# Where a norm weight is multiplied in: weight rows or transposed activations, in a two-layer decoder trunk

## The chip, the cores and the metric

One core of a Trainium2 chip runs the whole trunk in one launch. The metric is the device time of that core in microseconds. The engines are TensorE (PE, its weight loads PEld), VectorE (DVE), ScalarE (ACT), GpSimd (POOL) and SyncE (SP), which only issues DMAs here.

## The reference, cut to what matters

256 tokens of width 2048 pass two layers. Each sub-layer is `x += RMSNorm(f(RMSNorm(x)))`: a mixer (one input projection, attention in 8 + 8 heads of two kinds, one output projection) and a SwiGLU with 5632 hidden columns.

```python
def rms_norm(x, w):
    y = x * lax.rsqrt(jnp.mean(x * x, axis=-1, keepdims=True) + NORM_EPS)
    return y * w

for layer in range(2):
    u = rms_norm(h, mix_norm_pre[layer])
    u = mixer(u)                       # u @ w_in, two kinds of attention, @ w_out
    h = h + rms_norm(u, mix_norm_post[layer])
    u = rms_norm(h, ffn_norm_pre[layer])
    u = (silu(u @ w_gate) * (u @ w_up)) @ w_down
    h = h + rms_norm(u, ffn_norm_post[layer])
```

A norm in front of a projection is a factor per token (the rsqrt) and a weight per input column. `(x * r * w) @ W` is `r * (x @ (w * W))`, with w down the rows of W, and as well `r * ((x * w) @ W)`.

## The kernel before, in words

The 256 tokens are two tiles of 128. A projection takes the activations as the stationary operand, transposed to [128 k, 128 tokens], and streams weights past them as [128 k, 512 columns]. The products are exact to float32: both operands are split into a high part (rounded to float32r) and a low part (what is left), and `step` (L201 to L214) issues three matmuls per k tile, xh*wh (L208), xh*wl (L209), xl*wh (L210).

Weights come in pieces of two k tiles, 512 KB, one DMA on SP's queue each (`load_until`, L187 to L199). There are 808 of them: 120 in the first input projection (16 of these narrow, 272 or 256 columns), 96 in the second, 32 in each output projection, 528 in the two feed-forwards, of which 176 are of the down projection. For each k tile of a piece `split` (L177 to L184) makes the high part on ACT and the low part on DVE. Where the projection has a norm ahead of it (input, gate and up projections: 568 pieces) the norm weight, a column `nw` of one value per partition, is multiplied in on both engines (L183, L184); otherwise the plain forms are used (L180, L181). Raw pieces have 4 buffers, split pieces 10 (WB).

`transposed` (L251) makes the left operand of a normed projection: PE transposes a [128, 512] chunk of the residual into PSUM (L175), and one plain split of 512 columns follows (L180, L181, seen as m<-p). It runs for 8 chunks at the start, and from `post_residual` (L293) for 4 chunks of each tile at three turns: output projection to feed-forward (twice) and first feed-forward to second input projection. The factor per token (`prenorm_factor`, L260) is applied to the product.

Order of the work: `run_phase` (L231) emits pieces for tile 0 and tile 1 in turn, tile 1 some 4 pieces behind, 8 at both ends of a phase, so that what lies between two projections of one tile can run while PE works on the other. The attention arithmetic is cut into generators, whose steps are emitted between pieces (`advance`). Over this order a scheduler in the framework (`schedule_with_timeline_sim=True`, in `kernel`) plans each engine's own order by a timing model; on the chip every engine then keeps its order, and waits on semaphores.

Of the kernel before, what the change touches and what calls it, by code (L numbers as in the profile page):

```python
"""Two-layer hybrid decoder trunk (stick-breaking + gated DeltaNet, MoBA + dilated, SwiGLU) on one core.

Every projection runs on the tensor engine in float32r with both operands split exactly into a high
and a low part (x = xh + xl, w = wh + wl); xh*wh + xh*wl + xl*wh accumulate in float32 PSUM.
The activations are the stationary operand, transposed, [128 k, 128 tokens]; the weights stream past as
[128 k, 512 columns].  A norm in front of a projection costs no pass over the activations: its weight
goes into the rows of the projection as they are split, its factor into the product.
The 256 tokens are two tiles of 128; the second follows the first some weight pieces behind, so what
lies between two projections of one tile runs while the tensor engine works on the other.  The
attention arithmetic is emitted in small steps between weight pieces.  # L10
"""
# [6 lines left out]
F32R = mybir.dt.float32r  # L18
# [26 lines left out]
class Step:  # L45
    """One weight piece ([128, 2 k tiles, up to 512 columns]) and where it is used.  norm: the norm whose
    weight, one value per row of the piece, goes into it."""

    def __init__(self, src, kts, chunk, first, last, norm):
        self.src, self.kts, self.chunk, self.first, self.last, self.norm = src, kts, chunk, first, last, norm  # L50
        self.wh = self.wl = None


class Chunk:
    def __init__(self, pieces, lhs, done, norm=None):
        self.lhs, self.done = lhs, done
        self.acc = [None, None]
        n = len(pieces)
        self.steps = [Step(s, k, self, i == 0, i == n - 1, norm) for i, (s, k) in enumerate(pieces)]
# [9 lines left out]
class Pool:  # L69
    """Equal places handed out and returned in the order of the trace, each as a new tile.  # L70
    Requests of the generators are served in turn."""
# [26 lines left out]
    def renew(self, a):  # L98
        """The same place as a new tile."""
        return self.at(self.place.pop(id(a))[1])  # L100


def v4(t):
    """[128, 512] -> [128, 4, 128]"""
    return t.rearrange("p (h d) -> p h d", d=P)


class Builder:
# [23 lines left out]
    def now(self, pool, n=1):  # L132
        """Tiles for work that is emitted in one go."""
        while len(pool.free) < n:
            assert self.advance(), "no tile becomes free"
        return pool.pop(n)

    def bc(self, col, n=P):
        """[128, h] columns -> [128, h, n] with stride 0 on the last axis."""
        return col.unsqueeze(2).broadcast_to([P, col.shape[1], n])  # L140

    def rep(self, m, h=4):
        """[128, n] -> [128, h, n] with stride 0 on the middle axis."""
        return m.unsqueeze(1).broadcast_to([P, h, m.shape[1]])

    def rsqrt(self, v, n, tag):
        """v ** -0.5 for a [128, n] tile: a power and one Newton step, as two factors."""
# [12 lines left out]
    def rms(self, ss):  # L160
        """Sums of squares of four column chunks, and D * EPS beside them -> rms ** -1 as two factors."""
# [10 lines left out]
    def transpose4(self, o, src):  # L172
        """[128, 4, 128] -> [128, 512] with each [128, 128] block transposed."""
        for j in range(4):
            self.nc.tensor.transpose(o[:, j * P:(j + 1) * P], src[:, j, :], self.ident)  # L175

    def split(self, h, l, src, scale=None):  # L177
        """src (float32), times a column if there is one -> h (its float32r part) and l (what is left of it)."""
# [8 lines left out]
    def load_until(self, n):  # L187
        nc = self.nc
        while self.loaded < min(n, len(self.steps)):
# [5 lines left out]
            for j, kt in enumerate(s.kts):  # L195
                scale = None if s.norm is None else self.nw[:, s.norm * KT + kt:s.norm * KT + kt + 1]
                self.split(wh[:, j], wl[:, j], raw[:, j], scale)
# [18 lines left out]
    def advance(self):  # L216
        """Emits the next stage of each piece of attention work that can go on."""
# [13 lines left out]
    def run_phase(self, lo, hi, end):  # L231
        """Tile 1 follows LAG_EDGE pieces behind at both ends of a phase and LAG pieces in between."""
# [16 lines left out]
    # A norm in front of a projection: its weight is multiplied into the rows of the projection, its  # L249
    # factor (one per token) into the product.  # L250
    def transposed(self, t, c):  # L251
        """Column chunk c of the residual, transposed and split, as left operand."""
# [3 lines left out]
        self.split(h.bitcast(F32R), l.bitcast(F32R), o)  # L256
# [16 lines left out]
    def norm_weight(self, w, which, layer, c):  # L273
        """Columns of a norm weight, the same on every partition."""
# [18 lines left out]
    def post_residual(self, t, last):  # L293
        """x += y * rsqrt(mean(y^2)); y already holds the weight."""
# [6 lines left out]
        for c in range(4):  # L301
# [3 lines left out]
            if last:  # L305
                nc.sync.dma_start(out=self.out[t * P:(t + 1) * P, c * 512:(c + 1) * 512], in_=x)
            else:
                self.transposed(t, c)
        self.y[t] = None
        if not last:  # L310
# [6 lines left out]
    def run(self):  # L317
# [23 lines left out]
        for c in range(4):  # L341
            for t in range(2):
                self.transposed(t, c)
# [8 lines left out]
    def warm_up(self):  # L352
        """Products of zeros, until the first operands have arrived: the tensor engine's clock rises with use."""
# [15 lines left out]
    def ld_r(self, name, w):  # L369
        """w matrices of 0, 1 and -1 as float32r, which holds them exactly."""  # L370
# [25 lines left out]
    def col_chunk(self, w, c, done, norm):  # L396
        return Chunk([(w[c, p], (2 * p, 2 * p + 1)) for p in range(KT // 2)], self.lhs_a, done, norm)

    def plan_even_in(self):
# [5 lines left out]
        for g in range(2):  # L405
            for kind in (0, 1, 3, 2):
                if g == 0 and kind == 3:
                    chunks.append(self.col_chunk(self.I["ev_w_abz"], 0, lambda t, acc: self.abz_chunk(t, acc), 0))
                    chunks.append(self.col_chunk(self.I["ev_w_z"], 0, lambda t, acc: self.z_chunk(t, 0, 2, acc), 0))
                    continue  # L410
                done = lambda t, acc, g=g, kind=kind: self.gdn_chunk(t, g, kind, acc)
                chunks.append(self.col_chunk(w, c, done, 0))
                c += 1
            for kind in range(3):
                done = lambda t, acc, g=g, kind=kind: self.attn_chunk(t, 0, g, kind, acc)
                chunks.append(self.col_chunk(w, c, done, 0))
# [3 lines left out]
    def plan_odd_in(self):  # L420
        chunks = []
        for c in range(12):
            g, kind = c // 3, c % 3
            done = lambda t, acc, g=g, kind=kind: self.attn_chunk(t, 1, g, kind, acc)
            chunks.append(self.col_chunk(self.I["od_w_in"], c, done, 1))
# [16 lines left out]
    def plan_ffn(self, layer):  # L442
        chunks, waiting = [], []
        g, u, d = self.I["ffn_w_gate"], self.I["ffn_w_up"], self.I["ffn_w_down"]
        for q, grp in enumerate(FFN_GROUPS):
# [6 lines left out]
            for i, f in enumerate(grp):  # L452
                chunks.append(self.col_chunk(g[layer], f, lambda t, acc: self.gate_chunk(t, acc), 2 + layer))
                if i == 0:
                    chunks += waiting
                chunks.append(self.col_chunk(u[layer], f, lambda t, acc, i=i: self.up_chunk(t, i, acc), 2 + layer))
# [51 lines left out]
    def end_ffn(self, t, layer):  # L508
        self.post_residual(t, layer == 1)
# [40 lines left out]
    def end_out(self, t, layer):  # L550
        self.post_residual(t, False)

# [38 lines left out]
    def stick(self, t, g):  # L591
        """Weights are built transposed, [key, (head, query)]; the suffix sums over keys are products
        with triangular and all-ones matrices of the split terms."""
# [48 lines left out]
    def softmax_attn(self, t, g):  # L642
        """Causal softmax attention; the mask adds the logarithm of how often a key counts."""
# [51 lines left out]
    def abz_chunk(self, t, acc):  # L695
        """Columns a, b and the first two heads of z."""
# [31 lines left out]
    # The tokens of the second two heads of a group are in reverse order (flipped) in k, v and all that  # L728
    # is indexed like them: what is lower triangular in the first two heads is upper triangular there, and
    # one matrix holds both for the inverse.  Queries and outputs are in natural order throughout.  # L730
    def gdn_gates(self, t, ab):
        """The decay logs g [128, 8] split, beta [128, 8], exp of the prefix (tile 1) or suffix (tile 0) sums
        of g, and the prefix sums again in natural order."""
# [35 lines left out]
    def gdn_decay(self, t, g):  # L769
        """exp(sum of g over (k, c]) as [c, (head, k)] for k < c and as [k, (head, c)] for k <= c."""  # L770
# [30 lines left out]
    def gdn_conv(self, t, g, kind, nat):  # L801
        """Causal 4-tap convolution with the channels on partitions."""
# [6 lines left out]
        # heads, the columns of their tokens, of the taps before this tile and of the tile's last tokens  # L809
# [296 lines left out]
```

## Time and profile before

| | |
|---|---|
| time, median of 3 runs | 2433.02 us (2432.94 to 2434.01) |
| span of the profiled execution, first to last instruction | 2436.3 us, 3.3 us over that median |
| mean granted TensorE clock | 0.994 of full speed |
| PE busy | 2407.8 us |
| DVE busy | 1470.4 us |
| ACT busy | 1291.9 us |
| POOL busy | 194.7 us |
| chain of work that ended last | PE 94%, DVE 2%, ACT 1%, POOL 1%, DMA 1% |

Of the profiled execution the page gives its span as the only time; no other is listed for it. "Busy" is the time in which an engine runs at least one instruction. In a row of instructions, `out<-in` are tile names with buffer numbers left out: `wh`, `wl` are the high and low parts of a weight piece, `raw` the loaded piece, `m` one of the general [128, 512] tiles, `p` a PSUM tile, `acc` the accumulator of a projection, `nw` the norm weights. What stands behind the bar or in brackets is the idle time before and what ended it.

### The profile page before, as it was taken

What the parts mean: (1) busy time and instruction counts of PE and PEld (TensorE: products, weight loads), DVE (VectorE), ACT (ScalarE), POOL (GpSimd) and SP (SyncE); (2) the same over time, 40 slices, a digit from 0 to 9 for tenths busy, and PEclk for the clock granted to TensorE, in tenths of its full rate; (3) what the DMA queues carried; (4) which work ended last, traced back from release to release, by engine and by line L of the source; (5) the groups of instructions that cost most, each with busy time, mean ns of one, the idle gap of its engine ahead of it and who ended that gap; (6) DMA issues with size and microseconds to landing.
All of it is one profiled execution on the core that took longest, in us unless ns stands there. A gap on an engine that the chain in (4) does not pass through costs nothing.

```text
span 2436.3 us, 30747 instructions
## 1 busy us (share of the span) xinstructions
PE 2407.8 (99%) x11076; PEld 1968.3 (81%) x11076; DVE 1470.4 (60%) x2479; ACT 1291.9 (53%) x2270; POOL 194.7 (8%) x212
## 2 busy tenths in 40 slices
PE   9999999999999999999999999999999999999998
PEld 7888878888888888888887888888888888888886
DVE  7775876576555555555566565556555556555555
ACT  6664664565544545454555555556554544445443
POOL 0440470200000000000020000000000000000002
PEclk9999999999999999999999999999999999999999
DMA  7644444456555555555565445664555555555553
GB/s 239 208 143 152 132 145 152 147 178 213 185 186 186 186 186 183 189 189 182 193 211 199 166 174 173 202 198 159 206 188 184 186 187 188 182 190 182 185 196 129
DMA packets 128089, 441.99 MB, mean 181 GB/s; under 512 B 14848, under 2 KB 20224, under 8 KB 127936
## 3 DMA queue, kind: packets, MB, share of 16 engines
q1 hardware_dynamic: 121856, 425.91, 51.7%
q0 software_dynamic: 3920, 12.85, 1.8%
q8 instruction: 87, 1.43, 0.2%
q10 hardware_dynamic: 2160, 1.27, 0.2%
q14 instruction: 66, 0.54, 0.1%
HBM read 435.77 MB, written 4.19 MB: 181 GB/s over the span
## 4 chain that ended last, share of the span: by engine, by line
PE 94%; DVE 2%; issue 1%; ACT 1%; POOL 1%; DMA 1%; SPq 0%; POOLq 0%; DVEq 0%; ACTq 0%
PE acc L210 29%; PE acc L208 29%; PE acc L209 29%; PE p L175 2%; DVE wl L184 1%; PE p L931 1%; DMA raw<-in_ev_w_in 1%; PE p L659 0%; PE p L686 0%; PE p L940 0%; ACT wh L183 0%; PE p L604 0%; PE p L636 0%; DMA raw<-in_od_w_in 0%; POOL m L837 0%
## 5 line engine op out<-in xcount | busy, mean ns | idle before, releaser
L208 PE MATMUL acc<-wh,m 128*128 128x512 f32 (+1 forms) x3232 | 1275.8, 395 | 4.3 <-ACT m L180 4.3
L209 PE MATMUL acc<-wl,m 128*128 128x512 f32 (+1 forms) x3232 | 1272.5, 394 | 0.0
L210 PE MATMUL acc<-wh,m 128*128 128x512 f32 (+1 forms) x3232 | 1269.7, 395 | 1.7 <-DVE m L181 1.7
L184 DVE SCALAR_TENSOR_TENSOR wl<-raw,nw,wh 128x512 fp32r<-128x512 f32 (+2 forms) x1136 | 821.5, 760 | 542.8 <-ACT wh L183 541.0
L183 ACT ACTIVATE wh<-raw,nw 128x512 fp32r<-128x512 f32 (+2 forms) x1136 | 751.4, 710 | 604.9 <-PE acc L210 566.4
L208 PEld LDWEIGHTS acc<-wh,m 128*128 128x128 f32 x3232 | 609.2, 188 | 141.0 <-ACT m L180 5.1
L210 PEld LDWEIGHTS acc<-wh,m 128*128 128x128 f32 x3232 | 608.7, 188 | 141.3 <-DVE m L181 2.1
L209 PEld LDWEIGHTS acc<-wl,m 128*128 128x128 f32 x3232 | 608.7, 188 | 138.7
L181 DVE TENSOR_TENSOR wl<-raw,wh 128x512 fp32r<-128x512 f32 x480 | 313.7, 695 | 219.4 <-ACT wh L180 217.1
L180 ACT ACTIVATE wh<-raw 128x512 fp32r<-128x512 f32 x480 | 275.7, 624 | 248.4 <-PE acc L210 237.9
L276 POOL DMA_DIRECT2D m<-in_ffn_norm_post x16 | 9.0, 564 | 1393.2 <-PE acc L210 686.2
L495 DVE TENSOR_TENSOR m<-m,acc 128x512 f32<-128x512 f32 x80 | 54.7, 684 | 50.2 <-PE acc L210 50.2
L175 PE MATMUL p<-ident,m 128*128 128x128 f32 x528 | 78.1, 278 | 3.9 <-ACT m L873 3.5
L175 PEld LDWEIGHTS p<-ident,m 128*128 128x128 f32 x528 | 65.6, 144 | 17.5 <-ACT m L873 4.2
L181 DVE TENSOR_TENSOR m<-p,m 128x512 fp32r<-128x512 f32 x76 | 51.1, 689 | 44.0 <-ACT m L180 44.0
L180 ACT ACTIVATE m<-p 128x512 fp32r<-128x512 f32 x76 | 43.4, 596 | 52.8 <-PE p L175 52.8
L289 ACT ACTIVATE m<-m 128x512 f32<-128x512 f32 x48 | 30.0, 625 | 52.4 <-DVE m L495 37.7
L468 ACT ACTIVATE m<-acc,pr 128x512 f32<-128x512 f32 x44 | 30.4, 691 | 38.6 <-PE acc L210 38.0
L477 DVE SCALAR_TENSOR_TENSOR m<-acc,pr,m 128x512 f32<-128x512 f32 x44 | 32.9, 747 | 14.7 <-PE acc L210 14.7
L560 ACT ACTIVATE m<-acc,pr 128x512 f32<-128x512 f32 x36 | 24.8, 689 | 23.3 <-PE acc L210 22.8
L845 DVE SCALAR_TENSOR_TENSOR m<-c,conv,m 128x128 f32<-128x128 f32 x96 | 28.8, 344 | 0.0
L314 POOL DMA_DIRECT2D m<-xd x8 | 4.3, 543 | 271.3 <-DVE m L181 227.9
(199 smaller groups left out, 850.5 us busy)
## 6 DMA issues: line engine op xcount, KB each, us to landing
raw<-in_ffn_w_gate SPq DMA_DIRECT2D x176, 512.0 KB, 3.2
raw<-in_ffn_w_up SPq DMA_DIRECT2D x176, 512.0 KB, 3.2
raw<-in_ffn_w_down SPq DMA_DIRECT2D x176, 512.0 KB, 3.3
raw<-in_ev_w_in SPq DMA_DIRECT2D x104, 512.0 KB, 3.7
raw<-in_od_w_in SPq DMA_DIRECT2D x96, 512.0 KB, 3.3
raw<-in_ev_w_out SPq DMA_DIRECT2D x32, 512.0 KB, 4.3
raw<-in_od_w_out SPq DMA_DIRECT2D x32, 512.0 KB, 4.4
m<-in_mix_norm_post POOLq DMA_DIRECT2D x16, 256.0 KB, 5.1
```

The costliest lines, as they stand in the source:

```text
L175: self.nc.tensor.transpose(o[:, j * P:(j + 1) * P], src[:, j, :], self.ident)
L180: self.nc.scalar.activation(h, src, AF.Copy)
L181: self.nc.vector.tensor_sub(l, src, h.bitcast(F32))
L183: self.nc.scalar.activation(h, src, AF.Copy, scale=scale)
L184: self.nc.vector.scalar_tensor_tensor(l, src, scale, h.bitcast(F32), op0=ALU.mult, op1=ALU.subtract)
L208: nc.tensor.matmul(acc, xh, s.wh[:, j], start=(s.first and j == 0), stop=False)
L209: nc.tensor.matmul(acc, xh, s.wl[:, j], start=False, stop=False)
L210: nc.tensor.matmul(acc, xl, s.wh[:, j], start=False, stop=(s.last and j == 1))
L289: done = self.nc.scalar.activation(junk, src, AF.Square, accum_out=acc)
L468: self.nc.scalar.activation(self.sg[t], acc, AF.Silu, scale=self.r[t])
L477: nc.vector.scalar_tensor_tensor(u, acc, self.r[t], u, op0=ALU.mult, op1=ALU.mult)
L495: nc.vector.tensor_add(y, y, acc)
```

## The change

The norm weight is no longer given to the weight pieces. A piece is split by one plain ACTIVATE and one plain TENSOR_TENSOR over both k tiles (1024 columns). `transposed` gets the number of the norm, and splits its chunk in four parts of 128 columns, each with its column of `nw` as the scale. Comments and docstrings fall away as well.

```diff
-    def __init__(self, src, kts, chunk, first, last, norm):
+    def __init__(self, src, kts, chunk, first, last):
...
             nc.sync.dma_start(out=raw, in_=s.src)
-            for j, kt in enumerate(s.kts):
-                scale = None if s.norm is None else self.nw[:, s.norm * KT + kt:s.norm * KT + kt + 1]
-                self.split(wh[:, j], wl[:, j], raw[:, j], scale)
+            self.split(wh, wl, raw)
...
-    def transposed(self, t, c):
+    def transposed(self, t, c, norm):
         o = self.now(self.ps)
         self.transpose4(o, v4(self.x[t][c]))
         h, l = self.now(self.mem, 2)
-        self.split(h.bitcast(F32R), l.bitcast(F32R), o)
+        for j in range(4):
+            s = slice(j * P, j * P + P)
+            i = norm * KT + 4 * c + j
+            self.split(h.bitcast(F32R)[:, s], l.bitcast(F32R)[:, s], o[:, s], self.nw[:, i:i + 1])
...
-    def post_residual(self, t, last):
+    def post_residual(self, t, norm):
...
-            if last:
+            if norm is None:
                 nc.sync.dma_start(out=self.out[t * P:(t + 1) * P, c * 512:(c + 1) * 512], in_=x)
             else:
-                self.transposed(t, c)
+                self.transposed(t, c, norm)
...
-                self.transposed(t, c)
+                self.transposed(t, c, 0)
...
-        self.post_residual(t, layer == 1)
+        self.post_residual(t, None if layer else 1)
...
-        self.post_residual(t, False)
+        self.post_residual(t, 2 + layer)
```

## Rows read from the trace of the kernel before

**Rows 1.** The page, busy time of each engine.
```profile
PE 2407.8 (99%) x11076; PEld 1968.3 (81%) x11076; DVE 1470.4 (60%) x2479; ACT 1291.9 (53%) x2270; POOL 194.7 (8%) x212
```
**Rows 2.** Stretches: length, busy us of PE, PEld, DVE, ACT, POOL, clock, DMA.
```profile
30.00:440.00 410.00, 396.99 (x2116) 336.03 (x2115) 300.96 (x656) 248.32 (x508) 139.48 (x117) 0.98 0.49 156
440.00:1250.00 810.00, 810.00 (x3566) 655.66 (x3565) 463.47 (x709) 414.55 (x681) 16.60 (x26) 1.00 0.55 188
1250.00:1290.00 40.00, 37.58 (x162) 29.95 (x161) 33.26 (x60) 24.55 (x51) 9.54 (x13) 0.96 0.70 224
1290.00:2398.00 1108.00, 1108.00 (x4992) 901.21 (x4991) 638.75 (x986) 575.79 (x972) 15.45 (x29) 1.00 0.55 186
```
**Rows 3.** PE's waits: line, releaser, us in total, times, longest.
```profile
PE acc L208 <- ACT m L180: 4.3, 3, 3.2
PE p L931 <- POOL m L916: 3.6, 2, 2.3
PE p L175 <- ACT m L873: 3.5, 1, 3.5
PE p L940 <- ACT m L955: 3.1, 3, 2.0
PE p L763 <- DVE g L752: 2.1, 1, 2.1
PE acc L210 <- DVE m L181: 1.7, 1, 1.7
```
**Rows 4.** Stretch after the pause at 95 us, columns as in rows 2.
```profile
98.00:102.00 4.00, 4.00 (x14) 3.19 (x14) 4.00 (x4) 2.04 (x5) 3.90 (x4) 0.57 0.63 204
```
**Rows 5.** Groups by line and shape: busy us, mean ns; idle before.
```profile
L184 DVE SCALAR_TENSOR_TENSOR wl<-raw,nw,wh 128x512 fp32r<-128x512 f32 x1104 | 806.6, 768 | 542.8 <-ACT wh L183 541.0
L183 ACT ACTIVATE wh<-raw,nw 128x512 fp32r<-128x512 f32 x1104 | 736.9, 716 | 597.8 <-PE acc L210 562.6 <-issue 12.0 <-DMA raw<-in_ev_w_in 9.3
...
L181 DVE TENSOR_TENSOR m<-p,m 128x512 fp32r<-128x512 f32 x76 | 51.1, 689 | 44.0 <-ACT m L180 44.0
L180 ACT ACTIVATE m<-p 128x512 fp32r<-128x512 f32 x76 | 43.4, 596 | 52.8 <-PE p L175 52.8
...
L183 ACT ACTIVATE wh<-raw,nw 128x256 fp32r<-128x256 f32 x16 | 7.3, 501 | 3.2 <-PE acc L210 2.6 <-ACT c L822 0.5
...
L914 DVE SCALAR_TENSOR_TENSOR m<-p,gc,m 128x128 f32<-128x128 f32 x16 | 4.5, 342 | 0.0
```
**Rows 6.** Timeline of a quiet piece: start, us, engine, instruction, count.
```profile
899.95 1.42 DVE L184 SCALAR_TENSOR_TENSOR wl<-raw,nw,wh 128x512 fp32r<-128x512 f32 x2 [1.39 <-ACT wh L183]
901.98 1.34 ACT L183 ACTIVATE wh<-raw,nw 128x512 fp32r<-128x512 f32 x2 [1.45 <-PE acc L210]
```
**Rows 7.** The turn to the second input projection, columns as in rows 2.
```profile
1266.00:1288.00 22.00, 19.58 (x86) 15.41 (x85) 20.92 (x41) 16.77 (x34) 3.87 (x7) 0.92 0.64 208
```
**Rows 8.** Timeline of DVE ahead of the gates' products.
```profile
93.31 3.05 DVE L184 SCALAR_TENSOR_TENSOR wl<-raw,nw,wh 128x512 fp32r<-128x512 f32 x2
```
**Rows 9.** Timeline of DVE ahead of the second L916.
```profile
337.93 5.62 DVE L184 SCALAR_TENSOR_TENSOR wl<-raw,nw,wh 128x512 fp32r<-128x512 f32 x4 [11.67 <-ACT wh L183]
```
**Rows 10.** Timeline of POOL, 296 to 350 us.
```profile
297.00 9.45 POOL L825 COPY halo<-c 128x6 f32<-128x6 f32 x2 [1.61 <-ACT c L822]
...
313.41 8.40 POOL L793 TENSOR_TENSOR m<-m,gt_lt 128x512 f32<-128x512 f32 x1
...
322.04 3.02 POOL L837 TENSOR_TENSOR m<-c,conv 128x512 f32<-128x512 f32 x2
...
334.83 2.05 POOL L837 TENSOR_TENSOR m<-c,conv 128x512 f32<-128x512 f32 x2
```
**Rows 11.** L184 alone in a stretch: length, DVE busy and count, clock, DMA.
```profile
297.00:321.00 24.00, 12.16 (x17) 1.00 0.49 156
```
**Rows 12.** Timeline of DVE at the turn.
```profile
1275.29 5.76 DVE L184 SCALAR_TENSOR_TENSOR wl<-raw,nw,wh 128x512 fp32r<-128x512 f32 x7
```
**Rows 13.** The stretch of the Silu wait, columns as in rows 2.
```profile
313.00:349.00 36.00, 32.46 (x160) 26.96 (x159) 22.14 (x32) 23.93 (x50) 34.70 (x26) 0.95 0.43 142
```

More of the change, by code (lines that the diff above doesn't have):

```diff
@@ L45, with __init__ @@
 class Step:
-    def __init__(self, src, kts, chunk, first, last, norm):
-        self.src, self.kts, self.chunk, self.first, self.last, self.norm = src, kts, chunk, first, last, norm
+    def __init__(self, src, kts, chunk, first, last):
+        self.src, self.kts, self.chunk, self.first, self.last = src, kts, chunk, first, last
         self.wh = self.wl = None
 class Chunk:
-    def __init__(self, pieces, lhs, done, norm=None):
+    def __init__(self, pieces, lhs, done):
         self.lhs, self.done = lhs, done
@@ L58, in __init__ @@
         n = len(pieces)
-        self.steps = [Step(s, k, self, i == 0, i == n - 1, norm) for i, (s, k) in enumerate(pieces)]
+        self.steps = [Step(s, k, self, i == 0, i == n - 1) for i, (s, k) in enumerate(pieces)]
 def trunk(tc, I, out):
@@ L304, in post_residual @@
             self.mem.give(y)
-            if last:
+            if norm is None:
                 nc.sync.dma_start(out=self.out[t * P:(t + 1) * P, c * 512:(c + 1) * 512], in_=x)
             else:
-                self.transposed(t, c)
+                self.transposed(t, c, norm)
         self.y[t] = None
-        if not last:
+        if norm is not None:
             self.prenorm_factor(t)
@@ L393, in load_constants, with col_chunk @@
         nc.scalar.dma_start(out=self.lev[1][:, :384], in_=I["lev"][:, 512:])
-    def col_chunk(self, w, c, done, norm):
-        return Chunk([(w[c, p], (2 * p, 2 * p + 1)) for p in range(KT // 2)], self.lhs_a, done, norm)
+    def col_chunk(self, w, c, done):
+        return Chunk([(w[c, p], (2 * p, 2 * p + 1)) for p in range(KT // 2)], self.lhs_a, done)
     def plan_even_in(self):
@@ L407, in plan_even_in @@
                 if g == 0 and kind == 3:
-                    chunks.append(self.col_chunk(self.I["ev_w_abz"], 0, lambda t, acc: self.abz_chunk(t, acc), 0))
-                    chunks.append(self.col_chunk(self.I["ev_w_z"], 0, lambda t, acc: self.z_chunk(t, 0, 2, acc), 0))
+                    chunks.append(self.col_chunk(self.I["ev_w_abz"], 0, lambda t, acc: self.abz_chunk(t, acc)))
+                    chunks.append(self.col_chunk(self.I["ev_w_z"], 0, lambda t, acc: self.z_chunk(t, 0, 2, acc)))
                     continue
                 done = lambda t, acc, g=g, kind=kind: self.gdn_chunk(t, g, kind, acc)
-                chunks.append(self.col_chunk(w, c, done, 0))
+                chunks.append(self.col_chunk(w, c, done))
                 c += 1
@@ L415, in plan_even_in @@
                 done = lambda t, acc, g=g, kind=kind: self.attn_chunk(t, 0, g, kind, acc)
-                chunks.append(self.col_chunk(w, c, done, 0))
+                chunks.append(self.col_chunk(w, c, done))
                 c += 1
@@ L424, in plan_odd_in @@
             done = lambda t, acc, g=g, kind=kind: self.attn_chunk(t, 1, g, kind, acc)
-            chunks.append(self.col_chunk(self.I["od_w_in"], c, done, 1))
+            chunks.append(self.col_chunk(self.I["od_w_in"], c, done))
         return chunks
@@ L452, in plan_ffn @@
             for i, f in enumerate(grp):
-                chunks.append(self.col_chunk(g[layer], f, lambda t, acc: self.gate_chunk(t, acc), 2 + layer))
+                chunks.append(self.col_chunk(g[layer], f, lambda t, acc: self.gate_chunk(t, acc)))
                 if i == 0:
                     chunks += waiting
-                chunks.append(self.col_chunk(u[layer], f, lambda t, acc, i=i: self.up_chunk(t, i, acc), 2 + layer))
+                chunks.append(self.col_chunk(u[layer], f, lambda t, acc, i=i: self.up_chunk(t, i, acc)))
             waiting = down
```

## The prediction

> **What bounds the kernel now.** I read the busy shares first, then the stages, then who waits for whom, then the instructions around each wait. TensorE (PE) is busy 2407.8 us, 99% of the span, DVE 60% and ACT 53% of the span [rows 1]. By stage it is starker: in 440 to 1250 and in 1290 to 2398 us, the two feed-forwards, the output projections and the second input projection, PE is busy in every microsecond, and DVE is busy little over half of them [rows 2]. In these 1918 us a cheaper split on DVE or ACT is worth nothing, because PE's own work is the same before and after: the same products on the same sizes. Idle time of PE that lies next to the weight splits exists in two places alone: 410.00 - 396.99 = 13.0 us in the first input projection (30 to 440) and 40.00 - 37.58 = 2.4 us at the turn from the first feed-forward to the second input projection (1250 to 1290) [rows 2]. The rest of the 28.5 us is the start, before anything can run, and the tail, which has no weight pieces left.
>
> The waits of PE name the lost time [rows 3]: the products of the gates wait 2.1 us once for DVE; L931, the inverse, 3.6 us in two waits for POOL; a transpose 3.5 us for ACT's Silu, which itself waited for POOL; L940 3.1 us in three waits for ACT; at the turn 1.7 us for DVE's split of the transposed activations, and of L208's 4.3 us about 1.1 us (3.2 us is the start).
>
> [...]
>
> **The change, part by part.** Of the 808 weight pieces of two k tiles 568 carry a norm weight: 552 are full ones (1104 split instructions per engine [rows 5]) and 16 narrow; 240 carry none.
>
> *Removed and replaced.* A normed piece costs ACT two ACTIVATEs, 1.34 us together, and DVE two SCALAR_TENSOR_TENSORs, 1.42 us [rows 6]. After, each engine has one instruction of 1024 columns, which the trace doesn't show. From 256 to 512 columns the mean rises from 501 to 716 ns on ACT, from 128 to 512 columns from 342 to 768 ns on DVE [rows 5], so 512 columns more cost 0.43 and 0.57 us. Started from the plain forms, which the new ones are (0.596 and 0.689 us for 512 columns), that is 1.03 and 1.26 us; started from the scaled forms 1.15 and 1.34; two instructions as they are now are the other end, 1.34 and 1.42. I take 1.09 and 1.26, near the plain form: 0.25 us of ACT and 0.16 us of DVE saved per normed piece, 142 and 91 us in all. Nearly all of it is hidden under PE, as said. A matmul of the first k tile now waits for the whole piece, 0.4 to 0.6 us longer than for half of it; up to ten pieces are held ready, so this shows at the start alone, where the single instruction (1.09) ends before the second ACTIVATE did.
>
> *Added.* 32 chunks of transposed activations (8 at the start and 8 at each of three turns) are split by four scaled instructions of 128 columns per engine instead of one of 512. DVE's nearest row is sixteen such in 4.5 us, 1.12 for four [rows 5], against 0.689: +0.43. On ACT 128 columns come by the slope above to 0.39, the first whole and three more at about 0.29, 1.26 us in all against 0.596: +0.66; the ends are 1.0 and 4 x 0.50 = 2.0 us. A turn thus gains 8 x 0.43 = 3.4 us of DVE and 5.3 of ACT. DVE is busy 20.92 of 22.00 us at the turn to the second input projection [rows 7], so there is little room; but a piece comes every 3.0 us (2407.8 / 808), some seven in these 22 us, and they give back 7 x 0.16 = 1.1 of the 1.7 us that tile 0's four chunks add. And the first k tile is ready after about 0.3 instead of 0.69 us, while PE takes 3.0 / 4 = 0.7 us for a k tile of one token tile: once begun, the chain stays ahead. I put 0.7 us for all turns together; if the cover fails, see the rivals.
>
> *Moved.* No DMA and no queue is moved; a raw buffer comes free 0.16 us earlier, so SP issues its loads a little earlier.
>
> *What the stalls give back.* (1) Gates: behind POOL instructions two DVE splits took 3.05 us instead of 1.42 [rows 8]; one instruction meets POOL once, not twice, which saves half of the 1.6 us excess, and pieces ahead of it 0.16 each: 1.3 of the 2.1 us. (2) The two waits on POOL's L916: ahead of the second one four splits took 5.62 us [rows 9], where twice 1.42 would be 2.84; two instructions instead of four save half of the excess, 1.4, and I take 1.0 per wait: 2.0 of 3.6. (3) The Silu wait: POOL's copy of six columns and then a product stood 9.45 and 8.40 us [rows 10] while DVE's instructions followed one another without pause; 17 instructions of 297 to 321 us were weight splits [rows 11], 8.5 pieces, so the runs shorten by 1.4; I take 1.2 of 3.5. (4) L940: pieces there carry no norm, 0.3. (5) The turn: seven splits in 5.76 us [rows 12] stand ahead of the activations' split; 3.5 pieces save 0.6, the shorter first k tile 0.4, ACT's piece and chunk 0.5: 1.5 of 2.8 us. (6) With waits this much shorter I let two of five low-clock stretches go: 3.4 us. Sum 1.3 + 2.0 + 1.2 + 0.3 + 1.5 + 3.4 = 9.7, less 0.7: **9.0 us**. The sum is made against the profiled execution, span 2436.3 us, which is 3.3 us above the median of the timed runs (2433.0); I carry the difference over: 2424.0 us.
>
> **The rivals.** *Nothing shows (0.22).* Stalls 1 to 3 are POOL's and the loads' lateness and stay as long as they are; the order of the instructions on each engine is planned anew, and new small waits take the place of old ones. For it speaks that POOL is busy 34.70 of 36.00 us from 313 to 349 [rows 13], whatever DVE does. Then 1.5 us of the turn remain: 2431.5 us.
>
> *DVE holds POOL up for longer (0.07).* In the trace a POOL product that takes 1.03 us alone takes 1.5 beside DVE's splits (two in 3.02, against two in 2.05 [rows 10]), a wait of 0.48, over half of a 0.77 us split. Beside instructions of 1.26 us the same share is 0.79, so +0.31 for each POOL instruction that meets one. 26 POOL instructions lie ahead of the second Silu and L916 [rows 13] and as many ahead of the first; if two thirds meet a split and stand on PE's path, that is 17 x 0.31 = 5.3 us twice, 10.6. What I gave (1) to (3) is then lost, and 1.5 + 0.3 + 1.7 - 0.7 = 2.8 stays (the turn, L940 and one stretch of low clock): 2433.0 + 10.6 - 2.8 = 2441 us. The sign turns once one in five of them does, and it shows once half do; against it, a piece meets POOL once instead of twice.
>
> [...]
>
> *The turns overflow (0.05).* If DVE's 3.4 us and ACT's 5.3 us at each of three turns meet no gap, PE waits 2 us and loses 1.7 us of clock at each: +11.1, less the 4.8 of (1) to (4) and one stretch: 2433.0 + 11.1 - 6.5 = 2438 us.
>
> **How the numbers follow.** Forecast 0.66, the others as given. A measurement of this kernel tells about 0.2%, 4.9 us, from no change. Faster (under 2428.2) takes the forecast but for 0.04 at its shallow end: 0.62. Those 0.04, the no-show case and 0.01 of the turns make same, 0.27; the rest of the turns and POOL's case make slower, 0.11. The forecast's own range is 2413 to 2429: all five low stretches gone and 12 of 15 us of idle on one side, half the sum on the other. The range of 8 in 10 reaches through the no-show case, 2412 to 2437.
>
> **What would show it.** Weight splits after at 1.03 to 1.34 us each, DVE busy less by 60 to 100 us and ACT by 110 to 160; PE still busy throughout 440 to 1250 and 1290 to 2398; PE's idle time in 30 to 440 down from 13 to 7 or 8 us, at the turn under 1.5; three low-clock stretches. I am wrong if PE has new waits at any of the three turns, if POOL's products in 313 to 349 us get longer, or if the single DVE instruction takes 1.42 or more.

## The result, and the profile after

The change makes the kernel slower: 2456.65 us median (4 runs, 2455.95 to 2457.01) against 2432.98 us, a ratio of 1.0095 [1.0081, 1.0109], +23.7 us where -9.0 had been forecast. It lies outside the forecast's own range, 2413 to 2429 us, and outside the range of 8 in 10.

What the change was to do for DVE and ACT it does. The page after, busy times and the groups of the new instructions:

```profile
PE 2415.8 (98%) x11076; PEld 1969.2 (80%) x11076; DVE 1359.1 (55%) x1767; ACT 1137.3 (46%) x1558; POOL 189.5 (8%) x212
...
L180 DVE TENSOR_TENSOR wl<-raw,wh 128x1024 fp32r<-128x1024 f32 (+1 forms) x808 | 990.7, 1229 | 854.9 <-ACT wh L179 852.9
L179 ACT ACTIVATE wh<-raw 128x1024 fp32r<-128x1024 f32 (+1 forms) x808 | 848.6, 1051 | 956.9 <-PE acc L207 924.9
...
L182 ACT ACTIVATE m<-p,nw 128x128 fp32r<-128x128 f32 x128 | 38.6, 376 | 14.3 <-PE p L174 8.7
...
L183 DVE SCALAR_TENSOR_TENSOR m<-p,nw,m 128x128 fp32r<-128x128 f32 x128 | 38.0, 343 | 6.7 <-ACT m L182 6.3
```

Against [rows 1] DVE loses 111.3 us and ACT 154.6. PE, which sets the time, does the same work and is busy 8.0 us longer, at a mean granted clock of 0.992 where it was 0.994. Where it stands still is in its waits (the line numbers of after: L205 to L207 are the products, L174 the transposes, L932 the inverse, L941 the old L940):

```profile
PE acc L205 <- ACT m L182: 10.4, 9, 3.4
PE p L932 <- POOL m L917: 7.7, 2, 3.9
PE acc L207 <- DVE m L183: 4.1, 7, 0.9
PE p L941 <- DVE m L950: 2.2, 1, 2.2
PE p L941 <- ACT m L956: 1.3, 2, 0.8
...
PE p L913 <- ACT c L823: 0.9, 1, 0.9
PE p L174 <- ACT m L874: 0.6, 1, 0.6
```

Against [rows 3], PE waits 14.5 us in 16 waits for quarters (L182, L183), where it waited 6.0 us in 4 for the splits of whole chunks, the start among both; the inverse waits 7.7 us instead of 3.6, and the Silu wait of 3.5 us is down to 0.6 and 0.9. The stretches of after, columns as in [rows 2], then three of them behind the waits at the turns:

```profile
30.00:440.00 410.00, 395.96 (x2108) 334.82 (x2107) 272.27 (x536) 217.76 (x380) 126.67 (x114) 0.98 0.51 155
440.00:1250.00 810.00, 807.19 (x3542) 651.95 (x3542) 428.56 (x450) 360.33 (x423) 15.64 (x24) 1.00 0.57 186
1250.00:1310.00 60.00, 56.98 (x249) 45.01 (x248) 40.80 (x85) 35.67 (x81) 18.34 (x19) 0.94 0.60 200
1310.00:2398.00 1088.00, 1085.44 (x4865) 881.23 (x4865) 572.98 (x610) 485.82 (x596) 12.88 (x24) 1.00 0.56 184
...
536.00:541.00 5.00, 4.16 (x11) 2.99 (x12) 5.00 (x16) 3.51 (x12) 0.00 (x0) 0.66 0.57 197
1290.00:1299.00 9.00, 7.13 (x18) 4.33 (x18) 9.00 (x30) 6.60 (x20) 2.99 (x5) 0.62 0.77 285
1693.00:1702.00 9.00, 8.04 (x21) 5.63 (x22) 7.55 (x25) 5.57 (x18) 0.81 (x2) 0.62 0.40 147
```

PE has lost 2.8 us in 440 to 1250 and 2.6 us in 1310 to 2398, where before it was never idle [rows 2]: those are the first and the third turn. Behind each of the three turns the clock is at 0.62 to 0.66 of full speed for 5 to 9 us, a further 1.7 + 3.4 + 3.4 us (5 x 0.34 and twice 9 x 0.38).

What the turn looks like, the timeline of DVE after, at the first turn (PE's transposes of tile 0 run from 529.49 to 531.4 us):

```profile
530.41 1.22 DVE L180 TENSOR_TENSOR wl<-raw,wh 128x1024 fp32r<-128x1024 f32 x1
531.55 0.86 DVE L183 SCALAR_TENSOR_TENSOR m<-p,nw,m 128x128 fp32r<-128x128 f32 x3
...
532.67 1.23 DVE L180 TENSOR_TENSOR wl<-raw,wh 128x1024 fp32r<-128x1024 f32 x1
533.81 0.35 DVE L183 SCALAR_TENSOR_TENSOR m<-p,nw,m 128x128 fp32r<-128x128 f32 x1
...
534.81 0.61 DVE L183 SCALAR_TENSOR_TENSOR m<-p,nw,m 128x128 fp32r<-128x128 f32 x2
...
535.39 1.22 DVE L180 TENSOR_TENSOR wl<-raw,wh 128x1024 fp32r<-128x1024 f32 x1
536.53 0.61 DVE L183 SCALAR_TENSOR_TENSOR m<-p,nw,m 128x128 fp32r<-128x128 f32 x2
```

and PE's products that waited there:

```profile
533.78 0.50 PE L205 MATMUL acc<-wh,m 128*128 128x512 f32 x1 [0.98 <-ACT m L182]
...
535.21 0.50 PE L207 MATMUL acc<-wh,m 128*128 128x512 f32 x1 [0.69 <-DVE m L183]
536.11 0.50 PE L205 MATMUL acc<-wh,m 128*128 128x512 f32 x1 [0.41 <-ACT m L182]
...
537.58 0.79 PE L207 MATMUL acc<-wh,m 128*128 128x512 f32 x1 [0.73 <-DVE m L183]
```

The first four quarters (three at 531.55, one at 533.81) are not the four of one chunk: in the planned order, as the program is built, they are the first of each of the four chunks. PE takes the k tiles in order, so its second k tile is the fifth quarter, ready at 535.2 us, 3.3 us behind the first.

The start pays too. PE waits there 6.1 us for quarters, the first wait of 3.4 us and three later ones, where before it waited 3.2 us once for whole splits [rows 3]:

```profile
19.39 0.50 PE L205 MATMUL acc<-wh,m 128*128 128x512 f32 x1 [2.03 <-ACT m L182]
```

### The profile page after: what moved, and what is told of

Its sections match the earlier page's. It is cut to its first block, busy times and chain, and to the rows that moved or that the text cites. A ratio compares the mean times of both kernels' runs of the same rounds, so it can differ in the third digit from the quotient of the medians.

```text
span 2454.2 us, 29318 instructions
## 1 busy us (share of the span) xinstructions
PE 2415.8 (98%) x11076; PEld 1969.2 (80%) x11076; DVE 1359.1 (55%) x1767; ACT 1137.3 (46%) x1558; POOL 189.5 (8%) x212
## 4 chain that ended last, share of the span: by engine, by line
PE 90%; POOL 2%; DVE 2%; issue 2%; DMA 2%; ACT 1%; POOLq 0%; ACTq 0%; DVEq 0%; SPq 0%
PE acc L207 28%; PE acc L205 28%; PE acc L206 28%; PE p L174 2%; POOL m L838 1%; POOL m L840 1%; PE p L932 1%; ACT wh L179 1%; DVE wl L180 0%; DVE m L304 0%; DMA raw<-in_ev_w_in 0%; PE p L660 0%; PE p L687 0%; PE p L941 0%; POOL m L501 0%
## 5 line engine op out<-in xcount | busy, mean ns | idle before, releaser
L180 DVE TENSOR_TENSOR wl<-raw,wh 128x1024 fp32r<-128x1024 f32 (+1 forms) x808 | 990.7, 1229 | 854.9 <-ACT wh L179 852.9
L179 ACT ACTIVATE wh<-raw 128x1024 fp32r<-128x1024 f32 (+1 forms) x808 | 848.6, 1051 | 956.9 <-PE acc L207 924.9
L205 PE MATMUL acc<-wh,m 128*128 128x512 f32 (+1 forms) x3232 | 1276.7, 396 | 10.7 <-ACT m L182 10.4
L207 PE MATMUL acc<-wh,m 128*128 128x512 f32 (+1 forms) x3232 | 1272.6, 396 | 4.1 <-DVE m L183 4.1
L205 PEld LDWEIGHTS acc<-wh,m 128*128 128x128 f32 x3232 | 609.5, 189 | 151.1 <-ACT m L182 14.2
L207 PEld LDWEIGHTS acc<-wh,m 128*128 128x128 f32 x3232 | 609.5, 189 | 147.3 <-DVE m L183 8.5
L174 PE MATMUL p<-ident,m 128*128 128x128 f32 x528 | 77.4, 275 | 1.0 <-ACT m L874 0.6
L174 PEld LDWEIGHTS p<-ident,m 128*128 128x128 f32 x528 | 64.5, 142 | 14.3 <-ACT m L874 1.3
L179 ACT ACTIVATE m<-p 128x512 fp32r<-128x512 f32 x44 | 26.3, 598 | 72.9 <-PE p L174 72.7
L180 DVE TENSOR_TENSOR m<-p,m 128x512 fp32r<-128x512 f32 x44 | 30.4, 691 | 44.1 <-ACT m L179 44.1
L182 ACT ACTIVATE m<-p,nw 128x128 fp32r<-128x128 f32 x128 | 38.6, 376 | 14.3 <-PE p L174 8.7
L183 DVE SCALAR_TENSOR_TENSOR m<-p,nw,m 128x128 fp32r<-128x128 f32 x128 | 38.0, 343 | 6.7 <-ACT m L182 6.3
L932 PE MATMUL p<-m,m 128*128 128x128 f32 x112 | 20.7, 303 | 8.2 <-POOL m L917 7.7
```

The lines of the kernel that those rows point to most:

```text
L179: self.nc.scalar.activation(h, src, AF.Copy)
L180: self.nc.vector.tensor_sub(l, src, h.bitcast(F32))
L182: self.nc.scalar.activation(h, src, AF.Copy, scale=scale)
L183: self.nc.vector.scalar_tensor_tensor(l, src, scale, h.bitcast(F32), op0=ALU.mult, op1=ALU.subtract)
L205: nc.tensor.matmul(acc, xh, s.wh[:, j], start=(s.first and j == 0), stop=False)
L207: nc.tensor.matmul(acc, xl, s.wh[:, j], start=False, stop=(s.last and j == 1))
```

## The experiments

Each time is the median of 4 to 11 runs, with its ratio to the kernel before and that ratio's 95% interval; "before" ran beside each and has medians from 2432.0 to 2433.0 us.

**Which half of the change costs.** The quarters alone, on the kernel before, with a scale of ones:

```diff
-        self.split(h.bitcast(F32R), l.bitcast(F32R), o)
+        for j in range(4):
+            s = slice(j * P, j * P + P)
+            self.split(h.bitcast(F32R)[:, s], l.bitcast(F32R)[:, s], o[:, s], self.ones)
```

> The kernel before (two scaled splits of 512 columns per piece), with only the other half of the change: each chunk of transposed activations is split in four parts of 128 columns, scaled by a column of ones. Theory Q (the quarters put ACT and DVE behind at the start and the turns, and PE waits there): 10 to 14 us over before, 2443 to 2447, with waits of PE on the quarter splits at all three turns. Theory W (the whole-piece instructions of 1.22 us hold POOL up, and PE waits for POOL in the first projection): within 4 us of before, 2430 to 2437.

2450.16 us, 1.0075 [1.0063, 1.0088]: +17.1, 3 us over theory Q's range, with its waits at all three turns. The whole pieces alone, on the kernel after:

```diff
-        for j in range(4):
...
+        self.split(h.bitcast(F32R), l.bitcast(F32R), o)
```

> The changed kernel with the activations split by one plain instruction of 512 columns per engine; the norm weight ahead of the projections is left out, so only the whole-piece weight splits of the change remain. Theory Q: no slower than before, 2424 to 2433, no wait of PE at the first and third turn. Theory W: 8 to 12 us over before, 2441 to 2445, with the waits on POOL's product ahead of the inverse at 3 us or more each, as in the changed kernel.

2440.22 us, 1.0030 [1.0018, 1.0042]: +7.2, 1 us short of theory W's range and with its sign, two waits for POOL of 3.8 us each. 17.1 + 7.2 = 24.3: both halves cost, and they add. Whether it is the width of the weight instructions, by two of 512 columns:

```diff
-            self.split(wh, wl, raw)
+            for j in range(2):
+                self.split(wh[:, j], wl[:, j], raw[:, j])
```

> The changed kernel with each weight piece split by two plain instructions of 512 columns per engine. Theory Q: within 4 us of the changed kernel, 2452 to 2460, the turns wait as they do there. Theory W: 8 to 12 us faster than the changed kernel, 2445 to 2449, the waits on POOL back to 3.6 us in all.

2455.92 us, 1.0098 [1.0084, 1.0112]: the same as after, so narrow instructions give nothing back. The waits are made up in another way, though: the Silu wait is 3.0 us again, and the inverse waits 6.5 us (more on it below). And the quarters replaced by one product and one split of 512 columns:

```diff
-        for j in range(4):
...
+        self.nc.vector.tensor_mul(v4(u), v4(o), self.bc(self.nw[:, i:i + 4]))
+        self.split(h.bitcast(F32R), l.bitcast(F32R), u)
```

> The changed kernel with the norm weight multiplied into a transposed chunk by one DVE product of 512 columns (the weights broadcast along the tokens), followed by one plain split of 512 columns per engine: 3 instructions per chunk instead of 8. Theory Q: most of the loss at the turns goes, 2440 to 2447. Theory W: 2452 to 2457, since the weight splits are unchanged.

2459.23 us, 1.0109 [1.0096, 1.0123]: my theory's number was missed by 12 us. The turns still stall (3.1, 5.3 and 3.1 us of waits), though nothing is cut in four. A chunk now goes DVE, ACT, DVE, once more through a queue than before; whether that step or the longer work on DVE stalls the turns here was not tested.

**Order or volume.** First the weight splits were put, in order alone, behind the second chunk's last quarter:

```diff
+            if self.behind:
+                with self.tc.issue_after(self.behind[0].ins), self.tc.issue_after(self.behind[1].ins):
+                    self.split(wh, wl, raw)
```

> The kernel after with one thing added: at the three turns the splits of the next weight pieces are put, in order alone, behind the last quarter of a token tile's second chunk, on ACT and DVE. No operation is added or left out. Theory O (the order is what costs at the turns: pieces of 1.06 and 1.22 us are planned in between the quarters, so that the activations advance by two k tiles per piece): PE's waits for quarters at the three turns and the low clock behind them mostly go, 2444 to 2448 us; what is left over the kernel before, 11 to 15 us, is POOL's wait, the start and little ones. Theory V (the volume counts: 3.4 us more of DVE and 5.3 us more of ACT at each turn, in whatever order): 2452 us or more.

> The kernel before with the activations' chunks split by four scaled operations of 128 columns (by ones, so the numbers stay) and the same order as in the pinned kernel: at a turn, weight splits stand behind the second chunk's last quarter. Unpinned, the same quarters gave 2450 us. Theory O (order): 2437 to 2442 us, the three stalls mostly gone. Theory V (volume): 2447 us or more.

2451.81 us, 1.0081 [1.0067, 1.0095], and 2446.79 us, 1.0062 [1.0050, 1.0075]: 4.8 and 3.4 us given back, a quarter to a half of what order was to give, and both times lie 0.2 us below theory V's bound: inconclusive. The waits had only moved: quarters no longer wait at the turns, but the transposes of tile 1 wait 2.3 to 3.9 us, at five of six places for its residual update (L311 and L313 of these kernels), which stood behind the pieces held back.

Then I looked at what ACT's instructions wait for in the program as it is built. Of one chunk (m_4724 is its high part, p_4719 its PSUM tile), with other chunks and pieces in between:

```
L182 ACTIVATE m_4724<-p_4719,nw 128x128 [waits PE]
...
L182 ACTIVATE m_4724<-p_4719,nw 128x128 [waits DVE]
...
L182 ACTIVATE m_4724<-p_4719,nw 128x128 [waits DVE]
...
L182 ACTIVATE m_4724<-p_4719,nw 128x128 [waits DVE]
```

ACT's second quarter carries a wait for DVE's first, though it reads and writes other columns. The two engines read one PSUM tile in turn, and the framework orders such reads: in two programs that were built but not run, the wait is gone when DVE reads a constant in place of p, and stays when it reads one in place of the high part. So emitted as ACT, DVE, ACT, DVE, a chunk is a chain of eight steps from engine to engine, and the scheduler fills the gaps with the other chunks and with pieces. In the program without the wait a chunk's four quarters stand together in both queues although they are emitted in pairs: it is the wait that takes them apart. What the wait guards against is not shown; no run here read a chunk without it.

The test is to emit four on ACT and then four on DVE, with no instruction more or less:

```diff
-        for j in range(4):
-            self.split(h.bitcast(F32R)[:, s], l.bitcast(F32R)[:, s], o[:, s], self.nw[:, i:i + 1])
+        for half in range(2):
+            for j in range(4):
+                if half == 0:
+                    self.nc.scalar.activation(a, o[:, s], AF.Copy, scale=w)
+                else:
+                    self.nc.vector.scalar_tensor_tensor(b, o[:, s], w, a.bitcast(F32), op0=ALU.mult, op1=ALU.subtract)
```

> The kernel after, with a chunk's four quarters emitted as four ACT instructions and then four DVE instructions, where the kernel after emits ACT, DVE, ACT, DVE and so on; no operation is added or left out. Theory P (ping-pong): emitted in pairs, ACT's quarter j+1 carries a wait for DVE's quarter j of the same chunk, so one chunk's quarters come one at a time, and the order that is planned for both engines goes round all four chunks before the second k tile of the first; emitted in fours the waits go and a chunk's quarters stand together. Then PE's waits for quarters at the three turns and their low clock go, 2440 to 2447 us. Theory V (volume: 3.4 us more of DVE and 5.3 us more of ACT per turn): 2451 us or more.

> The kernel before with scaled quarters (by ones) for the activations, as in the run that gave 2450 us, but emitted as four on ACT and then four on DVE. The volume on both engines is the same as there. Theory P: 2433 to 2439 us, the three stalls gone. Theory V: 2446 us or more.

2441.67 us, 1.0035 [1.0023, 1.0047], and 2431.54 us, 0.9992 [0.9984, 1.0001]. Of the 128 quarters on ACT 96 carry a wait for DVE in the program of the kernel after, and none in the program of fours. On the kernel after this order gives back 15.0 us, the start's added waits among them; on the kernel before the same quarters go from +17.1 us to nothing. The same volume in another order costs nothing: ping-pong it is. The kernel after with this order, the timeline of DVE at the first turn:

```profile
532.05 1.12 DVE L262 SCALAR_TENSOR_TENSOR m<-p,nw,m 128x128 fp32r<-128x128 f32 x4
...
533.22 1.12 DVE L262 SCALAR_TENSOR_TENSOR m<-p,nw,m 128x128 fp32r<-128x128 f32 x4
...
534.31 1.12 DVE L262 SCALAR_TENSOR_TENSOR m<-p,nw,m 128x128 fp32r<-128x128 f32 x4
```

and its stretches at the first and the third turn, PE busy throughout and the clock at full speed:

```profile
518.00:545.00 27.00, 27.00 (x133) 22.33 (x132) 21.47 (x49) 19.16 (x46) 3.66 (x6) 1.00 0.47 161
...
1680.00:1705.00 25.00, 25.00 (x123) 20.58 (x122) 20.28 (x60) 18.23 (x50) 3.45 (x4) 1.00 0.38 128
```

**The other 9 us.** That kernel keeps the two waits of 3.9 us for the inverse. Of its waits for quarters the start (3.2 us) and those of the second turn are left:

```profile
PE p L937 <- POOL m L922: 7.7, 2, 3.9
PE acc L205 <- ACT m L260: 4.4, 2, 3.2
```

First a bound from the side: whole pieces only where no norm is (output and down projections), on the kernel before:

```diff
+            if s.norm is None:
+                self.split(wh, wl, raw)
+            for j, kt in enumerate(s.kts if s.norm is not None else ()):
```

> The kernel before, with only the 240 pieces without a norm weight (output projections and the second halves of the feed-forwards) split by one 1024-column operation per engine. If whole pieces cost only through POOL and the attention work between pieces of the normed projections: 2430 to 2436 us, no difference. If whole pieces cost by a later first k tile wherever one is used: slower, 2438 us or more.

2435.11 us, 1.0014 [1.0005, 1.0023]: inside the range of no difference, but the interval runs from 1.2 to 5.6 us over before: nothing is gained, and some of the 7 us may lie here. Then the 256-column addition ahead of the inverse on DVE in place of POOL, in the kernel of whole pieces and in the kernel before:

```diff
-        nc.gpsimd.tensor_add(L_[:, :2 * P], L_[:, :2 * P], L_[:, 2 * P:])
+        nc.vector.tensor_add(L_[:, :2 * P], L_[:, :2 * P], L_[:, 2 * P:])
```

> The kernel with whole weight pieces and plain 512-column activation splits (norm weight left out; it gave 2440 us), with the one 256-column addition ahead of the triangular inverse moved from POOL to DVE. If the 7 us that whole pieces cost are this POOL instruction, which PE waits for twice (7.6 us and the low clock behind it): 2430 to 2435 us. If they lie elsewhere: 2438 us or more.

> The kernel before with the same addition on DVE and nothing else. Its two waits on POOL are 3.2 to 3.6 us in all: 2426 to 2430 us if they go and nothing takes their place, 2431 to 2434 us if another wait (the instructions of DVE queued ahead) takes it.

2436.28 us, 1.0015 [1.0006, 1.0024], and 2434.95 us, 1.0008 [1.0000, 1.0017]. Moving the addition gives back 4 of the 7 us, between the two expectations, and its waits only fall from 3.8 to 3.0 us; to the kernel before it gives nothing. What stands ahead of it, in the kernel after, the timeline of DVE and then of POOL (`gss` are row sums, `gry` their power -0.5):

```profile
134.70 0.15 DVE L893 TENSOR_SCALAR gss<-gss 128x8 f32<-128x8 f32 x1
...
139.90 1.01 DVE L154 TENSOR_TENSOR gra<-gry 128x8 f32<-128x8 f32 x1 [3.93 <-POOL gry L150]
140.95 1.22 DVE L155 TENSOR_TENSOR gra<-gra,gss 128x8 f32<-128x8 f32 x1
142.20 1.23 DVE L156 TENSOR_SCALAR gra<-gra 128x8 f32<-128x8 f32 x1
```

```profile
127.48 1.27 POOL L879 TENSOR_TENSOR m<-m,onorm 128x512 f32<-128x512 f32 x1 [1.01 <-ACT m L874]
129.46 3.04 POOL L838 TENSOR_TENSOR m<-c,conv 128x512 f32<-128x512 f32 x2 [0.70 <-ACT c L823]
...
134.81 2.08 POOL L838 TENSOR_TENSOR m<-c,conv 128x512 f32<-128x512 f32 x1
136.96 1.29 POOL L840 TENSOR_TENSOR m<-m,m 128x512 f32<-128x512 f32 x1
138.22 1.66 POOL L150 TENSOR_TENSOR gry<-gss,mhalf 128x8 f32<-128x8 f32 x1
...
142.10 1.30 POOL L840 TENSOR_TENSOR m<-m,m 128x512 f32<-128x512 f32 x1
145.81 1.64 POOL L917 TENSOR_TENSOR m<-m 128x256 f32<-128x256 f32 x1 [2.41 <-DVE m L915]
```

The same on POOL in the kernel before (its second profile, below):

```profile
134.11 2.02 POOL L151 TENSOR_TENSOR gry<-gss,mhalf 128x8 f32<-128x8 f32 x1 [0.51 <-DVE gss L892]
...
141.26 0.72 POOL L916 TENSOR_TENSOR m<-m 128x256 f32<-128x256 f32 x1 [2.62 <-DVE m L914]
```

Before, POOL waits for the sums, and starts the power at once. After, two products are still to be done when the sums are ready, and it starts 3.4 us behind them (134.85 to 138.22); DVE waits, and its three tiny instructions take over 1 us each beside POOL's, as two of the three do before (1.26 and 1.21 us). The cause is not a longer list: as the programs are built, one product fewer stands ahead of the power on POOL than before. POOL is late with it, behind two waits for ACT (127.48 and 129.46 above) and with products of 2.1 us. How much of the lateness each of these makes was not tested. So the power was taken off POOL:

```diff
-        nc.gpsimd.tensor_tensor(y, v, self.mhalf[:, :n], op=ALU.pow)
+        if tag == "gr":
+            nc.scalar.activation(a, v, AF.Ln)
+            nc.scalar.activation(y, a, AF.Exp, scale=-0.5)
```

> The kernel after with quarters in fours (2441.7 us), and the inverse square root of the attention's row sums (the 128x8 power) taken from POOL's queue: ACT computes it as a logarithm and an exponential. Theory K (queue: beside whole pieces POOL's products take longer and one pair more of them stands ahead of that power, which DVE waits for 3.9 us, and at its end PE for the 256-column addition): both waits of 3.9 us and the low clock behind them shrink, 2432 to 2437 us. Theory L (the waits are the addition's own 1.64 us on POOL and where PE's order has the product): 2440 us or more.

> The same with the 256-column addition on DVE too, so that nothing of POOL's is left in the chain to the triangular inverse. Theory K: 2429 to 2434 us, which would be the kernel before or a little under it. Theory L: 2436 to 2438 us, what the addition alone gives (it gave 4 us with plain activations).

> The kernel before with the power on ACT and nothing else. There the power starts 0.14 to 0.5 us after its sums, so both theories expect little: 2429 to 2434 us. It is the control for the two runs above: what it gains is not the change's.

2432.14 us, 0.9998 [0.9989, 1.0006]; 2431.19 us, 0.9993 [0.9985, 1.0002]; 2432.61 us, 1.0001 [0.9992, 1.0010]. The power on ACT gives back 9.5 us to the kernel with quarters in fours, and nothing to the kernel before: theory K, in that the power's place in POOL's queue is what costs. POOL's addition then ends at 143.1 instead of 146.5 us (in the kernel of quarters in fours), as its timeline shows:

```profile
142.38 0.72 POOL L926 TENSOR_TENSOR m<-m 128x256 f32<-128x256 f32 x1 [1.14 <-DVE m L924]
```

and PE's waits for it are what they were before:

```profile
PE p L941 <- POOL m L926: 3.6, 2, 1.8
```

The 9.5 us hold more than these two waits: those of the products behind the inverse (L941 of the kernel after) fall from 3.7 to 1.5 us with them, and the clock in 30 to 440 us is at 0.99 instead of 0.98. With weight splits of two narrow instructions (2455.92 us, above) the path is another:

```profile
136.25 1.96 POOL L150 TENSOR_TENSOR gry<-gss,mhalf 128x8 f32<-128x8 f32 x1 [0.26 <-DVE gss L894]
...
144.15 2.31 POOL L918 TENSOR_TENSOR m<-m 128x256 f32<-128x256 f32 x1 [2.41 <-DVE m L916]
```

There the power starts 0.14 us behind its sums, the sums themselves come later, and the addition takes 2.31 us beside the next splits; PE waits 6.5 us all the same. What would mend that kernel was not tested.

Moving the addition too gives no more. No version beats the kernel before by what can be told.

**Before, once more.**

> The kernel before once more, for a second profile: 2431 to 2436 us; the first profiled execution was about 5 us above its median. If the extra lies in one place (a low clock or a late load), the difference between the two profiles shows it.

A single run: 2429.82 us, span 2428.0 us. Its mean clock is 0.998, that of the first profile 0.994; in 30 to 440 us it reads

```profile
30.00:440.00 410.00, 399.58 (x2145) 338.11 (x2144) 303.80 (x668) 249.87 (x511) 132.16 (x118) 1.00 0.50 157
```

so 10.4 us of idle time at a clock of 1.00, against 13.0 us and 0.98 [rows 2], and no wait of the gates for DVE [rows 3]. The 8.3 us between the two spans of one kernel are of that kind.

## Why the prediction was wrong

The way back from 2456.65 to 2432.14 us has two steps: the order of the quarters, 15.0 us, and the power taken out of POOL's queue, 9.5 us. They are steps of one way, so that their sum, 24.5 against the 23.7 us lost, says no more than that its end is the time before. That both are losses of the change, and not gains of their own, the two controls on the kernel before show: quarters in fours 2431.54 us, the power on ACT 2432.61 us.

*What bounds the kernel: right.* The some 266 us that DVE and ACT no longer work are worth nothing: mended of both losses the kernel takes 2432.1 us, what it took before.

*The sizes of single instructions: right.* Weight splits 1.23 and 1.05 us (1.26 and 1.09 taken), four quarters 1.12 us on DVE and 1.23 on ACT (1.12 and 1.26 taken). DVE's busy time fell by 111.3 us, more than the 60 to 100 expected; the sum had counted savings on 568 of the 808 pieces. The 3.4 and 5.3 us more a turn fit in, as the run with quarters in fours shows.

*The step that failed* is "once begun, the chain stays ahead. I put 0.7 us for all turns together", an overlap that did not hold. It priced four instructions on each engine by their durations and let each engine run its own four back to back. In the order in which the loop emits them they are a chain of eight across two queues, whose second k tile comes 3.3 us behind the first, and not 0.3. The term measured 15.0 us, the start's some 3 us of added waits among them, where nothing had been put for the quarters. The diff showed the order of emission, and the rows of before showed that the split reads p on both engines [rows 5]; what neither shows is the wait that the framework puts between two such reads, since before each engine read a chunk once.

*Gain (2), the inverse,* had the wrong sign: +4.1 us of waits (3.6 to 7.7), and 9.5 us with the later waits and the low clock behind them (0.50 from 149 to 151 us in the kernel after), where -2.0 had been given. I counted how much sooner POOL would get in between DVE's instructions, not how late POOL would then come to the power that DVE itself waits for. *Gain (3), the Silu,* came and was undersized: 3.5 to 1.5 us, 2.0 instead of 1.2, with whole pieces; with two plain instructions to a piece it is 3.0. *Gains (4) and (5)* did not come: L940's 3.1 us are 3.5 in two lines after, and the turn to the second input projection still waits 2.7 us with the quarters in fours. Of the 2.8 us that the sum counted there, 0.3 are a wait of L208 at 422 us. *Gains (1) and (6)* were read from one execution: the second profile of the same kernel has no such wait of the gates, and its clock is 1.00 in 30 to 440 and in 1250 to 1290 us, where the first has 0.98 and 0.96 [rows 2]. The 1.7 us of a low-clock stretch, in (6) and in the rivals, are 4.00 x 0.43 [rows 4], and the first profile has five such stretches of 4 us, at 0.57 or 0.58, from 98, 334, 354, 412 and 1283 us. But that shorter waits let two of the five go, 3.4 us, no run shows. The second profile has its clocks of 1.00 with no change to the kernel, and after waits of nearly one length the clock fell in one run and not in another (last section).

*The rivals.* "The turns overflow" (+11.1) and "DVE holds POOL up for longer" (+10.6) named both places and both sizes nearly, and were given 0.05 and 0.07 as alternatives. Nothing excluded both; 2433.0 + 11.1 + 10.6 is 2454.7 us. The first had the wrong cause, volume; the second's, longer products on POOL, is at most a part of it, since the whole 9.5 us came back when the power alone left POOL.

## What to carry to other kernels

When an operation on one PSUM tile is cut into parts that two engines read in turn, in this framework, count the hand-overs and not the durations (15.0 us here): emit all parts of the one engine, then all of the other, and look in the built program at what each instruction waits for. Busy time saved on engines that PE covers was worth nothing here (some 266 us), while a new order of their queues cost 15.0 and 9.5 us at places where PE has no slack; two rivals at two places are to be added, not weighed against each other. Take a second profile of the kernel before, where the sum hangs on waits of a microsecond.

## What the hardware showed

With splits by TENSOR_TENSOR POOL's standstills of 9.45 and 8.40 us [rows 10] are gone (between 60 and 440 us no row of POOL's is over 3.1 us); instead a POOL product that meets one takes about 2.1 us (2.08 above), where alone it takes 1.03 [rows 10], and the reverse, DVE instructions of 8 columns take 1.01 to 1.23 us beside POOL's products of 1.05 to 1.30 us. In the second profile of before two of them take 1.26 and 1.21 us beside such products, and the third, which starts at 138.70 us when the last product has ended at 138.64, takes 0.17. The long standstills of before went through many instructions of DVE's: the one of 8.40 us began at 313.41 us within a row of them without a pause, from 311.87 to 320.67 us (DVE busy in 8.79 of these 8.80 us), and ended 1.1 us behind it; why POOL stood through all of them no run shows.

A pause of PE can cost twice. In the run with the quarters alone the stretch at the second turn reads, columns as in [rows 2],

```profile
1284.00:1296.00 12.00, 7.13 (x21) 4.36 (x20) 12.00 (x37) 8.82 (x26) 1.80 (x5) 0.72 0.81 269
```

4.9 us of waits, and 12 x 0.28 = 3.4 us of clock. It does not always. At the same turn, with quarters in fours, waits of 1.2 and 1.4 us were followed by no low clock; with the power on ACT besides, waits of 1.2 and 1.5 us were followed by 0.52 of full speed for 7 us:

```profile
1284.00:1300.00 16.00, 13.34 (x66) 10.78 (x66) 13.99 (x46) 12.05 (x42) 5.65 (x8) 1.00 0.71 253
...
1278.00:1285.00 7.00, 6.21 (x15) 4.91 (x16) 6.54 (x26) 3.93 (x13) 2.45 (x5) 0.52 0.59 213
```

So what a wait of this size costs in clock can't be told from its length alone.
